# Down-projections of a hybrid decoder by seven block products for eight, with operands loaded stage by stage

## The chip, the cores and the metric

The kernel runs on one core of a Trainium2 chip. The metric is the time of one execution on the device in microseconds (us), the median over several runs; beside it one execution was profiled, and every row below is from that one.

Names of the engines: PE (TensorE) does matmuls, PEld is its weight load, DVE (VectorE) and ACT (ScalarE) do elementwise work, POOL is GpSimd, SP only issues DMAs here. The clock that PE was granted is given as a share of 2.4 GHz.

## The reference

A decoder trunk of two layers on one sequence of 1024 positions and 1024 channels, in float32. Layer 0 mixes tokens by two convolutional groups, layer 1 by stick-breaking attention with 16 heads. Each layer ends with a gated feed-forward block, which is what the change is about:

```python
D_FF = 2816                                   # 22 blocks of 128 channels
def conv_ffn(h, w_up, dw_w, dw_b, w_down):
    u = causal_dwconv(h @ w_up, dw_w, dw_b)   # width 3, along positions
    gate, val = jnp.split(u, 2, axis=-1)
    return (jax.nn.silu(gate) * val) @ w_down # (1024, 2816) @ (2816, 1024)

h = rmsnorm(x, ffn_norm_g[layer])
x = x + conv_ffn(h, ffn_w_up[layer], ffn_dw_w[layer], ffn_dw_b[layer], ffn_w_down[layer])
```

The last product is the down-projection. It runs once in each layer.

## The kernel before

**Precision.** PE multiplies in a reduced format, so each operand is split in a high and a low part: `split` (L421 to 429) casts on ACT (L426) and subtracts on DVE (L427). `mm3` (L439 to 444) then makes three matmuls of 512 columns, high x high, high x low, low x high, into one PSUM bank.

**Memory.** SBUF is managed as slots of 128 x 1024 floats (`Mem`): 16 low slots, which lie in the two buffers `hH` and `hL` and are free only while the normed input isn't needed, and 38 others; an allocation asks for one kind or the other. PSUM has eight banks of 512 columns: three double tiles (`bigs`) and two single ones (`sms`).

**Up.** `Up.block(f)`, for f from 0 to 21, computes gate and value of one block of 128 channels by seven block products for eight, adds the convolution, and multiplies (`post`, L387 to 408). The result, a tile of 128 channels x 1024 positions, is stored to DRAM (`hd[f]`, L406). So the transposed activations of the down-projection lie in DRAM, 22 tiles.

**Down.** `ffn` (L935 to 1004) cuts the 22 blocks in groups of 3, 5, 5, 5 and 4 (`GROUPS`). For each group it loads the activations of a block (L950) and its weight rows (L951), both 128 x 1024, and splits them. `back_tile` goes over the eight row tiles of 128 positions: for each it sums all blocks of the group into a double bank by 2 x 3 matmuls per block, and adds the sum to the residual tile `x[t]` with one DVE instruction of 1024 columns (L576). While one group is multiplied the next is loaded and split, one block per row tile. The last group goes through `back_all` (L579 to 607), which calls the next layer's `tail` after each row tile, or stores the output rows. The residual tiles come back from DRAM all at once, before the first group (L970).

**Order.** Outside the first stage and the attention the framework's scheduler orders each engine's instructions by the times that it estimates for them. Each engine, and SP's queue of DMAs, then runs strictly in that order: an instruction that waits holds up all behind it on its engine. A DMA on SP's queue waits for the slot that it writes to be free, so for the last reader of what was there.

## Time and profile before

| | us |
|---|---|
| median of 3 runs (lowest to highest) | 2390.34 (2389.73 to 2393.57) |
| profiled execution | 2388.36 |
| its span, first to last instruction | 2386.6 |
| PE busy | 2291.5, 11340 matmuls |
| DVE busy | 1612.6 |
| ACT busy | 1186.9 |
| POOL busy | 570.8 |

A row of the page's groups gives the line in the kernel, the engine, the operation, what it writes and reads, how often, the busy time in us, the mean of one in ns, and then the engine's idle time just before, with what ended it. A window gives for each engine the busy us in it. Matmuls overlap, so the busy time of one (some 390 ns) is longer than the distance from one to the next.

In time order: the convolutional mixer ends at about 380; Up of layer 0 lasts to about 780, its down-projection to about 1010; the attention follows, to about 1660; Up of layer 1 lasts to about 2120, its down-projection to the end. The passage from an Up to its down-projection is called the ramp below.

### The profile page before, as it was taken

How to read it: one execution, taken by the hardware profiler on the slowest of the kernel's cores; microseconds unless marked ns; L12 is line 12 of the kernel's file. 1: busy time of each engine (PE TensorE's matmuls, PEld its weight loads, DVE VectorE, ACT ScalarE, POOL GpSimd, SP SyncE). 2: the span in 40 equal slices, each digit the busy share in tenths (PEclk: the TensorE clock that was granted, in tenths of full speed). 3: DMA queues.
4: the chain of work that ended last, by engine and by line, in shares of the span. 5: the costliest groups of instructions: out<-in, count | busy, mean ns of one | idle time of the engine just before them, and what ended most of it. 6: DMA issues, size and time to landing. Idle time of an engine off the chain costs nothing.

```text
span 2386.6 us, 29571 instructions
## 1 busy us (share of the span) xinstructions
PE 2291.5 (96%) x11340; PEld 1958.7 (82%) x11340; DVE 1612.6 (68%) x1772; ACT 1186.9 (50%) x1882; POOL 570.8 (24%) x555
## 2 busy tenths in 40 slices
PE   8998998999999899999999999989899999999999
PEld 8886886888888788899899999878688888877887
DVE  6779458777766744246888888886867766766332
ACT  5442336565555421026677767764655555543110
POOL 2221113121111000025555555651311111200000
PEclk9999999999999999999999999999999999999999
DMA  5983044666665632211111110224466666646211
GB/s 170 190 177 92 27 137 106 171 148 141 166 159 146 220 129 93 61 54 27 36 27 36 36 36 10 86 83 146 106 150 150 155 150 154 145 149 250 71 36 71
DMA packets 225056, 268.43 MB, mean 112 GB/s; under 512 B 10013, under 2 KB 168209, under 8 KB 224913
## 3 DMA queue, kind: packets, MB, share of 16 engines
q1 hardware_dynamic: 194385, 201.61, 25.8%
q0 software_dynamic: 30528, 64.92, 16.1%
q8 instruction: 89, 1.46, 0.3%
q14 instruction: 54, 0.44, 0.1%
HBM read 158.07 MB, written 43.52 MB: 84 GB/s over the span
## 4 chain that ended last, share of the span: by engine, by line
PE 65%; DVE 15%; DMA 7%; ACT 5%; issue 5%; POOL 3%; DVEq 0%; SPq 0%; POOLq 0%; ACTq 0%
PE ps2b L442 7%; PE ps2b L444 7%; PE ps2b L443 7%; PE ps0b L442 6%; PE ps0b L444 6%; PE ps0b L443 6%; DMA t<-t 4%; PE ps0bb L443 3%; PE ps0bb L442 3%; PE ps0bb L444 3%; DVE t L1125 3%; DVE t L427 2%; PE ps1s L442 2%; PE ps1s L443 2%; PE ps1s L444 2%
## 5 line engine op out<-in xcount | busy, mean ns | idle before, releaser
L426 ACT CAST t<-t 128x1024 fp32r<-128x1024 f32 x242 | 249.2, 1048 | 329.8 <-DMA t<-t 76.0
L427 DVE TENSOR_TENSOR t<-t,t 128x1024 fp32r<-128x1024 f32 x238 | 300.5, 1276 | 96.0 <-ACT t L426 72.4
L201 POOL DMA_DIRECT2D t<-t x176 | 155.4, 965 | 679.0 <-DMA t<-in_ffn_w_up_dram 200.3
L617 DVE SCALAR_TENSOR_TENSOR t<-t,cst,t 128x1023 f32<-128x1023 f32 (+1 forms) x184 | 236.9, 1288 | 77.2 <-ACT t L615 71.3
L1125 DVE TENSOR_TENSOR_SCAN t<-t 128x127 f32<-128x127 f32 (+7 forms) x128 | 205.6, 1613 | 8.3 <-ACT t L1116 7.9
L442 PE MATMUL ps2b<-t,t 128*128 128x512 f32 x516 | 202.0, 392 | 6.7 <-ACT t L426 2.6
L443 PE MATMUL ps2b<-t,t 128*128 128x512 f32 x516 | 201.3, 390 | 0.5 <-DVE t L427 0.5
L444 PE MATMUL ps2b<-t,t 128*128 128x512 f32 x516 | 201.1, 390 | 0.0
L508 POOL TENSOR_TENSOR stat<-stat,mhalf 128x8 f32<-128x8 f32 (+1 forms) x65 | 80.7, 1242 | 399.5 <-DVE stat L507 399.4
L442 PE MATMUL ps1s<-wH,hH 128*128 128x384 f32 x448 | 165.3, 369 | 0.0
L444 PE MATMUL ps0b<-hH,t 128*128 128x512 f32 x396 | 154.9, 391 | 3.4 <-DVE t L427 3.4
L442 PE MATMUL ps0b<-hH,t 128*128 128x512 f32 x396 | 156.2, 395 | 1.4 <-ACT t L334 1.4
L443 PE MATMUL ps0b<-hL,t 128*128 128x512 f32 x396 | 155.1, 392 | 0.0
L444 PE MATMUL ps1s<-wH,hL 128*128 128x384 f32 x448 | 150.9, 337 | 0.0
L443 PE MATMUL ps1s<-wL,hH 128*128 128x384 f32 x448 | 150.5, 336 | 0.0
L1130 POOL TENSOR_TENSOR t<-t,t 128x639 f32<-128x639 f32 (+1 forms) x64 | 108.5, 1696 | 174.9 <-DVE t L1125 102.4
L442 PE MATMUL ps0b<-t,t 128*128 128x512 f32 x362 | 142.0, 392 | 3.5 <-DVE t L576 3.5
L443 PE MATMUL ps0b<-t,t 128*128 128x512 f32 x362 | 141.3, 390 | 0.0
L444 PE MATMUL ps0b<-t,t 128*128 128x512 f32 x362 | 141.2, 390 | 0.0
L615 ACT ACTIVATE t<-t,cst 128x1024 f32<-128x1024 f32 x88 | 109.3, 1242 | 43.4 <-DVE t L375 27.9
L1116 ACT ACTIVATE t<-ps1s 128x512 f32<-128x512 f32 (+1 forms) x192 | 95.5, 497 | 55.7 <-PE ps1s L1112 28.0
L442 PEld LDWEIGHTS ps2b<-t,t 128*128 128x128 f32 x516 | 96.8, 188 | 30.5 <-ACT t L426 3.4
(316 smaller groups left out, 5880.9 us busy)
## 6 DMA issues: line engine op xcount, KB each, us to landing
t<-in_ffn_w_up_dram SPq DMA_DIRECT2D x88, 512.0 KB
t<-t POOLq DMA_DIRECT2D x176, 256.0 KB, 4.0
hd<-t SPq DMA_DIRECT2D x44, 512.0 KB
t<-hd SPq DMA_DIRECT2D x44, 512.0 KB
t<-in_ffn_w_down_dram SPq DMA_DIRECT2D x44, 512.0 KB
xd<-t SPq DMA_DIRECT2D x24, 512.0 KB
t<-xd SPq DMA_DIRECT2D x24, 512.0 KB
wr<-in_attn_w_qkv_dram SPq DMA_DIRECT2D x24, 512.0 KB
```

The costliest lines, as they stand in the source:

```text
L201: nc.gpsimd.dma_start(out=out, in_=src, accum_op=ALU.add)
L426: nc.scalar.copy(out=r(m.ap(h)), in_=m.ap(src))
L427: (eng or nc.vector).tensor_tensor(out=r(m.ap(l)), in0=m.ap(src), in1=m.ap(h), op=ALU.subtract)
L442: mm(out=ps, lhsT=sH, rhs=mH, start=start, stop=False, skip_group_check=onto)
L443: mm(out=ps, lhsT=sH, rhs=mL, start=False, stop=False, skip_group_check=onto)
L444: mm(out=ps, lhsT=sL, rhs=mH, start=False, stop=stop, skip_group_check=onto)
L508: nc.gpsimd.tensor_tensor(out=ss, in0=ss, in1=self.mhalf[:, 0:count], op=ALU.pow)
L615: nc.scalar.activation(dst, src, AF.Identity, scale=wcols[2], bias=bias)
L617: nc.vector.scalar_tensor_tensor(out=dst[:, s:], in0=src[:, :S - s], scalar=wcols[2 - s], in1=dst[:, s:], op0=ALU.mult, op1=ALU.add)
L1116: nc.scalar.activation(K[:, c0:c1], ps, AF.Sigmoid, scale=-sc)
L1125: self.nc.vector.tensor_tensor_scan(out=rev, data0=rev, data1=rev, initial=1.0, op0=ALU.mult, op1=ALU.bypass)
L1130: self.nc.gpsimd.tensor_tensor(out=B[:, 0:n - 1], in0=B[:, 0:n - 1], in1=K[:, 1:n], op=ALU.mult)
```

## The change

The 22 channel blocks are taken as 11 pairs, positions and output columns in halves. A pair's contribution is then a product of 2 x 2 blocks, and is made by seven block products with sums of blocks as operands (Winograd's form of Strassen's method). All pairs sum into the same banks, so the combinations of the products are made once, over all pairs.

- **Activations.** `post` hands its tile to the new `store`. For an even block it stores the first half and keeps the tile; for the odd one it makes four half-size sums on DVE and stores three tiles. `hs[i]` holds seven half tiles for each pair, in the order in which they are used, 1.75 MB instead of 1 MB.
- **Weights.** The sums of weight blocks are made in the down-projection, on DVE, in one slot per pair that stays for three stages.
- **Stages.** `Down` walks 4 stages x 11 pairs, 44 steps. Stages 1 to 3 make two products a step (banks `a[t]` and `d[t]`, t from 0 to 3), stage 4 makes one. `a` keeps accumulating over all four stages; `d` starts anew in stages 1 and 3. After the last pair of stages 1, 2 and 3 the eight banks are added to halves of `x` (`add`), after stage 4 the four of `a`.
- **Flow.** `ahead` issues loads three steps ahead and preparations (sums, casts, splits) two steps ahead. The residual tiles are loaded one per step, in steps 4 to 11 of stage 1. Split operands lie in the low slots, four per step, in stages 1 to 3.
- **Tails.** Row tiles 0 to 3 are complete after stage 3, and their tails run in the first steps of stage 4; tiles 4 to 7 follow one by one at the end, for which the last six pairs are multiplied tile by tile. In layer 1 halves of rows are stored as they are complete.
- **Attention.** `qkv_piece` takes its first bank from the third double tile.

The core of the diff:

```diff
-GROUPS = [3, 5, 5, 5, 4]
...
-        nc.sync.dma_start(out=k.hd[f], in_=m.ap(v))
-        for s in (g, sg, v):
+        for s in (g, sg):
+            m.free(s)
+        self.store(f, v)
+    def store(self, f, v):
+        k, m, nc = self.k, self.k.m, self.k.nc
+        hs = k.hs[f // 2]
+        lo, hi = slice(0, 512), slice(512, 1024)
+        if f % 2 == 0:
+            nc.sync.dma_start(out=hs[:, 0:512], in_=m.ap(v)[:, lo])
+            self.even = v
+            return
+        q = [m.alloc() for _ in range(2)]
+        E, O, S12, S43 = [m.ap(s) for s in (self.even, v, *q)]
+        for out, x, y, op in ((S12[:, lo], E[:, hi], O[:, hi], ALU.add), (S12[:, hi], S12[:, lo], E[:, lo], ALU.subtract),
+                              (S43[:, lo], O[:, lo], S12[:, hi], ALU.subtract), (S43[:, hi], E[:, lo], E[:, hi], ALU.subtract)):
+            nc.vector.tensor_tensor(out=out, in0=x, in1=y, op=op)
+        for c, s in zip((512, 1536, 2560), (*q, v)):
+            nc.sync.dma_start(out=hs[:, c:c + 1024], in_=m.ap(s))
+        for s in (self.even, v, *q):
             m.free(s)
 
...
+class Down:
+    N = NF // 2
+    LOAD, PREP = 3, 2
+    OUTER = 5
...
+        self.steps = [(s, i) for s in range(4) for i in range(self.N)]
...
+        halves = [b[:, c:c + 512] for b in big for c in (0, 512)]
+        self.a, self.d = halves[0:4], halves[4:6] + sm
...
+    def load(self):
+        s, i = self.steps[self.nl]
+        self.nl += 1
+        k, m, sync = self.k, self.k.m, self.k.nc.sync
+        lo = slice(0, 512)
+        if s == 3 and i == 0 and self.l == 0:
+            m.held = set(range(NSLOT - NLAST, NSLOT))
+        n = 512 if s == 3 else 1024
+        a = m.alloc()
+        if s == 0:
+            self.w[i] = m.alloc(keep=True)
+        w = m.ap(self.w[i])
+        if s == 0:
+            sync.dma_start(out=w, in_=self.row0[i])
+        elif s == 1:
+            sync.dma_start(out=w[:, lo], in_=self.rows[i][3])
+        sync.dma_start(out=m.ap(a)[:, 0:n], in_=k.hs[i][:, s * 1024:s * 1024 + n])
+        b = None
+        if s == 2:
+            b = m.alloc()
+            sync.dma_start(out=w[:, lo], in_=self.rows[i][0])
+            sync.dma_start(out=m.ap(b)[:, lo], in_=self.rows[i][2])
+        self.raw[s, i] = a, b
+    def prep(self):
+        s, i = self.steps[self.np]
+        self.np += 1
+        k, m, nc = self.k, self.k.m, self.k.nc
+        lo, hi = slice(0, 512), slice(512, 1024)
+        a, b = self.raw.pop((s, i))
+        w = m.ap(self.w[i])
+        def sub(out, x, y):
+            nc.vector.tensor_tensor(out=out, in0=x, in1=y, op=ALU.subtract)
+        def split(src, ht):
+            h, l = m.alloc(ht), m.alloc(ht)
+            nc.scalar.copy(out=r(m.ap(h)), in_=src)
+            nc.vector.tensor_tensor(out=r(m.ap(l)), in0=src, in1=m.ap(h), op=ALU.subtract)
+            return h, l
+        def split_half(src):
+            s = m.alloc()
+            h, l = m.ap(s)[:, lo], m.ap(s)[:, hi]
+            nc.scalar.copy(out=r(h), in_=src)
+            nc.vector.tensor_tensor(out=r(l), in0=src, in1=h, op=ALU.subtract)
+            return s
+        if s == 3:
+            self.ops[s, i] = split_half(m.ap(a)[:, lo]), split_half(w[:, lo])
+            m.free(self.w.pop(i))
+        else:
+            x = split(m.ap(a), True)
+            if s == 0:
+                sub(w[:, hi], w[:, hi], w[:, lo])
+                y = split(w, True)
+            elif s == 1:
+                sub(w[:, hi], w[:, lo], w[:, hi])
+                y = split(w, True)
+            else:
+                B = m.ap(b)
+                sub(B[:, hi], w[:, hi], w[:, lo])
+                sub(w[:, lo], B[:, lo], w[:, hi])
+                y = split(B, True)
+                m.free(b)
+            self.ops[s, i] = (*x, *y)
+        m.free(a)
+    def products(self, s, i, t):
+        k, m = self.k, self.k.m
+        ops = [r(m.ap(o)) for o in self.ops[s, i]]
+        ts, lo, hi = slice(t * P, (t + 1) * P), slice(0, 512), slice(512, 1024)
+        first, last = i == 0, i == self.N - 1
+        if s == 3:
+            x, y = ops
+            k.mm3(self.a[t], x[:, ts], x[:, 512 + t * P:512 + (t + 1) * P], y[:, lo], y[:, hi], False, last, True)
+            return
+        xh, xl, yh, yl = ops
+        t2 = slice(512 + t * P, 512 + (t + 1) * P)
+        a, d = ((lo, hi), (hi, lo), (hi, lo))[s]
+        k.mm3(self.a[t], xh[:, ts], xl[:, ts], yh[:, a], yl[:, a], first and s == 0, last, s > 0)
+        k.mm3(self.d[t], xh[:, t2], xl[:, t2], yh[:, d], yl[:, d], first and s != 1, last, s == 1)
+    def add(self, t, c, ps):
+        x = self.k.m.ap(self.k.x[t])[:, c * 512:(c + 1) * 512]
+        self.k.nc.vector.tensor_tensor(out=x, in0=ps, in1=x, op=ALU.add)
...
+    def run(self):
+        k, m = self.k, self.k.m
+        k.x = [None] * NT
+        for n, (s, i) in enumerate(self.steps):
+            if s == 3 and i == self.OUTER:
+                break
+            self.ahead(n)
+            if s == 0 and i >= self.N - NT:
+                t = i - (self.N - NT)
+                k.x[t] = m.alloc(keep=True)
+                k.nc.sync.dma_start(out=m.ap(k.x[t]), in_=k.xd[t])
+            for t in range(4):
+                self.products(s, i, t)
+                if i == self.N - 1:
+                    to, c = ((0, 0), (0, 1), (4, 1))[s]
+                    self.add(t + to, c, self.a[t])
+                    to, c = ((4, 1), (0, 1), (0, 0))[s]
+                    self.add(t + to, c, self.d[t])
+            self.close(s, i)
+            if s == 2 and i == self.N - 1:
+                m.drop_ht()
+                if self.l:
+                    for t in range(4):
+                        self.tail(t + 4, slice(512, 1024))
+            if s == 3 and i < 4:
+                self.tail(i)
+        self.ahead(len(self.steps))
+        for t in range(4):
+            for i in range(self.OUTER, self.N):
+                self.products(3, i, t)
+            self.add(t + 4, 0, self.a[t])
+            if t == 3:
+                for i in range(self.OUTER, self.N):
+                    self.close(3, i)
+            if self.l == 0:
+                self.tail(t + 4)
+            else:
+                self.tail(t + 4, slice(0, 512))
...
+        down = Down(self, l, tail)
...
+                down.load()
...
+                down.load()
+                down.prep()
...
+        self.m.give_ht()
+        down.run()
...
-            self.qps = self.big()[:, 0:512] if p == 0 else self.qbs[t % len(self.qbs)]
+            self.qps = self.bigs[2][:, t % 2 * 512:(t % 2 + 1) * 512] if p == 0 else self.qbs[t % len(self.qbs)]
...
-            self.hd = [dp.tile([P, S], F32, name=f"hd{f}") for f in range(NF)]
+            self.hs = [dp.tile([P, 7 * 512], F32, name=f"hs{i}") for i in range(NF // 2)]
```

SP's queue of DMAs in the ramp of layer 0, before: `hd` and `xd` are the activations and residual tiles in DRAM, the number behind a name tells the tile (`hd_108` is block 0).

```order
L970 DMA t_5615<-xd_100 128x1024
L406 DMA hd_128<-t_5472 128x1024
L970 DMA t_5617<-xd_101 128x1024
L951 DMA t_5709<-in_ffn_w_down_dram 128x1024
L950 DMA t_5708<-hd_114 128x1024
L970 DMA t_5619<-xd_102 128x1024
L970 DMA t_5621<-xd_103 128x1024
L950 DMA t_5735<-hd_115 128x1024
L951 DMA t_5736<-in_ffn_w_down_dram 128x1024
L970 DMA t_5623<-xd_104 128x1024
L970 DMA t_5625<-xd_105 128x1024
L951 DMA t_5632<-in_ffn_w_down_dram 128x1024
```

The same place after: `hs_108` is pair 0, L475 loads activations, L472 the weights of stage 1, L474 a half row of weights for stage 2, L567 a residual tile.

```order
L475 DMA t_6130<-hs_113 128x1024
L474 DMA t_5543<-in_ffn_w_down_dram 128x512
L475 DMA t_5715<-hs_112 128x1024
L475 DMA t_6322<-hs_108 128x1024
L472 DMA t_5887<-in_ffn_w_down_dram 128x1024
L475 DMA t_5956<-hs_108 128x1024
L472 DMA t_5678<-in_ffn_w_down_dram 128x1024
L472 DMA t_5716<-in_ffn_w_down_dram 128x1024
L567 DMA t_5895<-xd_103 128x1024
L472 DMA t_5922<-in_ffn_w_down_dram 128x1024
L475 DMA t_6162<-hs_114 128x1024
L474 DMA t_5674<-in_ffn_w_down_dram 128x512
```

Before, residual tiles and the next blocks' operands alternate. After, among the loads of stage 1 stand those of later stages: `t_6130` and `t_6162` are activations of stage 2, `t_6322` of stage 3, and L474 writes a slot (`t_5543`, `t_5674`) that the stage 1 split of the same weights must have read.

DVE between two groups before: L576 adds a double bank to a row tile, L427 is the subtraction of a split.

```order
L427 TENSOR_TENSOR t_6358<-t_6287,t_6357 128x1024
L576 TENSOR_TENSOR t_5615<-ps0bb_559,t_5615 128x1024
L427 TENSOR_TENSOR t_6362<-t_6288,t_6361 128x1024
L576 TENSOR_TENSOR t_5617<-ps0b_71,t_5617 128x1024
L576 TENSOR_TENSOR t_5619<-ps0b_72,t_5619 128x1024
L576 TENSOR_TENSOR t_5621<-ps0bb_559,t_5621 128x1024
L576 TENSOR_TENSOR t_5623<-ps0b_71,t_5623 128x1024
L576 TENSOR_TENSOR t_5625<-ps0b_72,t_5625 128x1024
L576 TENSOR_TENSOR t_5627<-ps0bb_559,t_5627 128x1024
```

DVE at the end of stage 2 of layer 0 after: L551 adds one bank to half a row tile, L498 is the subtraction of a split, L493 a sum of weight blocks.

```order
L498 TENSOR_TENSOR hL<-t_6356,hL 128x1024
L498 TENSOR_TENSOR hL<-t_6358,hL 128x1024
L493 TENSOR_TENSOR t_6681<-t_5922 128x512
L493 TENSOR_TENSOR t_5922<-t_6681,t_5922 128x512
L551 TENSOR_TENSOR t_5790<-ps0b_71,t_5790 128x512
L498 TENSOR_TENSOR hL<-t_6391,hL 128x1024
L551 TENSOR_TENSOR t_5790<-ps0bb_548,t_5790 128x512
L498 TENSOR_TENSOR hL<-t_6393,hL 128x1024
L551 TENSOR_TENSOR t_5860<-ps0b_72,t_5860 128x512
L551 TENSOR_TENSOR t_5825<-ps0b_71,t_5825 128x512
L551 TENSOR_TENSOR t_5860<-ps0bs_549,t_5860 128x512
```

Eight adds of 512 columns stand where adds of 1024 columns were, in a place where all eight banks end together, with splits for stage 3 between them.

## Rows read from the trace of the kernel before

**Rows 1.** The page, part 1: busy us of each engine, share of the span, instructions.
```profile
PE 2291.5 (96%) x11340; PEld 1958.7 (82%) x11340; DVE 1612.6 (68%) x1772; ACT 1186.9 (50%) x1882; POOL 570.8 (24%) x555
```

**Rows 2.** Windows by stage; x counts the instructions that touch a window.
```profile
core 0: us, PE busy (x) PEld busy (x) DVE busy (x) ACT busy (x) POOL busy (x), PEclk, DMA share, GB/s
400.00:775.00 375.00, 374.72 (x1652) 309.23 (x1651) 265.53 (x256) 216.64 (x274) 66.44 (x76) 1.00 0.65 155
1740.00:2115.00 375.00, 373.64 (x1643) 307.60 (x1642) 265.05 (x256) 214.44 (x273) 66.24 (x76) 1.00 0.65 153
780.00:840.00 60.00, 53.37 (x229) 42.11 (x228) 47.43 (x42) 29.04 (x31) 0.00 (x0) 1.00 0.66 243
2115.00:2180.00 65.00, 59.59 (x256) 47.31 (x255) 50.86 (x46) 32.27 (x35) 0.00 (x0) 1.00 0.62 225
850.00:1000.00 150.00, 150.00 (x664) 124.20 (x663) 49.27 (x44) 19.99 (x24) 0.00 (x0) 1.00 0.17 59
2190.00:2370.00 180.00, 180.00 (x796) 149.08 (x795) 53.57 (x45) 18.23 (x18) 0.00 (x0) 1.00 0.14 51
```

**Rows 3.** Waits of TensorE in the two ramps: us in total, times, longest us.
```profile
PE ps0b L442 <- DVE t L576: 3.5, 3, 1.6
PE ps0bb L442 <- ACT t L426: 2.6, 2, 1.9
...
PE ps2b L442 <- ACT t L426: 2.6, 2, 1.9
PE ps2b L442 <- DVE t L576: 1.6, 2, 1.3
```

**Rows 4.** Groups by line: DVE and ACT in 780:840, then TensorE in 850:1000.
```profile
L427 DVE TENSOR_TENSOR t<-t,t 128x1024 fp32r<-128x1024 f32 x11 | 13.2, 1220 | 1.3 <-ACT t L426 1.3
L576 DVE TENSOR_TENSOR t<-ps0b,t 128x1024 f32<-128x1024 f32 x5 | 6.1, 1222 | 0.4 <-DMA t<-xd 0.4
L380 DVE TENSOR_TENSOR t<-t,t 128x512 f32<-128x512 f32 x1 | 0.7, 686 | 0.0
...
L426 ACT CAST t<-t 128x1024 fp32r<-128x1024 f32 x12 | 12.6, 1047 | 12.5 <-DMA t<-hd 4.3 <-DVE hH L427 3.2 <-DVE t L405 3.1
...
L442 PE MATMUL ps0b<-t,t 128*128 128x512 f32 x72 | 28.0, 389 | 0.0
```

**Rows 5.** Windows of 10 us, a DMA issue group of the page, a wait of SP.
```profile
770.00:780.00 10.00, 10.00 (x46) 8.28 (x45) 5.32 (x6) 3.94 (x4) 0.00 (x0) 1.00 0.07 27
790.00:800.00 10.00, 8.57 (x36) 6.79 (x37) 4.02 (x4) 1.44 (x2) 0.00 (x0) 1.00 0.32 110
810.00:820.00 10.00, 10.00 (x46) 8.28 (x45) 9.69 (x10) 6.75 (x7) 0.00 (x0) 1.00 0.99 386
2180.00:2190.00 10.00, 10.00 (x45) 8.27 (x45) 7.59 (x7) 3.66 (x4) 0.00 (x0) 1.00 1.02 410
...
t<-t POOLq DMA_DIRECT2D x176, 256.0 KB, 4.0
...
SPq L406 <- DVE t L405: 196.9, 41, 9.1
```

**Rows 6.** Timeline of the last row tile: start, length, engine, instruction.
```profile
2378.16 0.39 PE L444 MATMUL ps2b<-t,t 128*128 128x512 f32 x1
...
2378.58 0.69 DVE L602 TENSOR_TENSOR t<-ps2b,t 128x512 f32<-128x512 f32 x1 [1.49 <-PE ps2b L444]
2379.33 0.50 PE L442 MATMUL ps2b<-t,t 128*128 128x512 f32 x1 [0.78 <-DVE t L602]
```

**Rows 7.** The longest wait of TensorE in 375:405, and windows around it.
```profile
PE ps0bb L443 <- DVE t L427: 6.2, 1, 6.2
...
384.00:388.00 4.00, 0.49 (x1) 0.17 (x1) 4.00 (x3) 2.83 (x4) 4.00 (x2) 0.97 0.00 0
388.00:392.00 4.00, 1.33 (x3) 1.14 (x4) 4.00 (x3) 1.35 (x2) 1.53 (x1) 0.50 0.00 0
392.00:396.00 4.00, 4.00 (x14) 3.13 (x14) 3.82 (x5) 0.96 (x2) 0.00 (x0) 0.68 0.44 129
```

More of the change, by code (lines that the diff above doesn't have):

```diff
@@ L40 @@
 NLAST = 9
-GROUPS = [3, 5, 5, 5, 4]
-FILL = 2
 MOVED_TAPS = 10
@@ L414, in close, with __init__, ahead @@
                     self.k.m.free(s)
+class Down:
+    N = NF // 2
+    LOAD, PREP = 3, 2
+    OUTER = 5
+    def __init__(self, k, l, tail):
+        self.k, self.l, self.tail = k, l, tail
+        self.w, self.raw, self.ops = {}, {}, {}
+        self.steps = [(s, i) for s in range(4) for i in range(self.N)]
+        self.nl = self.np = 0
+        big, sm = k.bigs, k.sms
+        halves = [b[:, c:c + 512] for b in big for c in (0, 512)]
+        self.a, self.d = halves[0:4], halves[4:6] + sm
+        wd = k.a["ffn_w_down"][l]
+        self.rows = [[wd[f * P:(f + 1) * P, c:c + 512] for f in (2 * i, 2 * i + 1) for c in (0, 512)] for i in range(self.N)]
+        self.row0 = [wd[2 * i * P:(2 * i + 1) * P, :] for i in range(self.N)]
+    def load(self):
[60 more added lines that the diff above has]
+        m.free(a)
+    def ahead(self, n):
+        while self.nl < min(n + self.LOAD + 1, len(self.steps)):
+            self.load()
+        while self.np < min(n + self.PREP + 1, len(self.steps)):
+            self.prep()
+    def products(self, s, i, t):
[15 more added lines that the diff above has]
+        self.k.nc.vector.tensor_tensor(out=x, in0=ps, in1=x, op=ALU.add)
+    def close(self, s, i):
+        for o in self.ops.pop((s, i)):
+            self.k.m.free(o)
+    def run(self):
[36 more added lines that the diff above has]
+                self.tail(t + 4, slice(0, 512))
@@ L935, in ffn @@
     def ffn(self, l, tail):
-        m, nc = self.m, self.nc
         up = self.up
```

56 lines of the change are left out of this document (removed).

## The prediction

> **What bounds the kernel now.** I read the page's totals first, then windows by stage, then the waits of TensorE, then the durations. TensorE is busy for 96% of the span, and the next engine, DVE, for 68% [rows 1]. The windows show what that share is made of. Both Up stages run at 374.7 and 373.6 us busy of 375, and the inner parts of both down-projections at 150 of 150 and 180 of 180 us, with the granted clock at 1.00 [rows 2]. So in a down-projection every matmul taken away shortens the path, as long as nothing else becomes late. The exception is the passage from Up to down ("the ramp"): 53.4 of 60 us and 59.6 of 65 us are busy [rows 2]. TensorE loses 6.6 and 5.4 us there, in short waits, the longest of 1.9 us, for casts and for the adds that free PSUM [rows 3]. DVE is at 79% in those stretches and the DMA share at 0.66 and 0.62, against 0.17 and 0.14 later [rows 2]: that is the one place where other resources are nearly as full as TensorE.
>
> **The matmuls.** A down-projection is 22 channel blocks x 8 row tiles x 2 column halves x 3 = 1056 matmuls of 512 columns. The new one is 11 pairs x 4 tiles x 7 products x 3 = 924. So 132 go in each layer, 264 in all. In the steady stretch 796 start in 180 us, 0.2261 us each [rows 2]; the 389 ns of a single one [rows 4] overlap with their neighbours. 264 x 0.2261 = 59.7 us, all on the path: **-59.7**. Two blocks' products now go into one bank without further work, since a bank keeps accumulating from stage to stage.
>
> **DVE in steady state.** A split of a 128x1024 tile is a cast of 1.05 us on ACT and a subtraction of 1.22 us on DVE; a 128x512 tensor operation takes 0.69 us [rows 4]. A step of stage 1 or 2 needs two splits and one half-size subtraction: 2 x 1.22 + 0.69 = 3.1 us of DVE beside 24 matmuls = 5.4 us of TensorE. Stage 3 needs 3.8 of 5.4, stage 4 1.4 of 2.7. ACT needs 2.1 of 5.4. For a layer the splits, subtractions and 28 half-size adds sum to 145 us of DVE (before: 44 splits and 40 adds of 1.22 = 102.5) under 924 x 0.2261 = 209 us of TensorE. That is hidden, and costs nothing while DVE works ahead; preparation runs two steps ahead. Loads are 1.05 MB per 5.4 us step, 193 GB/s, where 386 and 410 GB/s were moved for 10 us at a time [rows 5]. Steady state: **0**.
>
> **The ramp.** Here the load queue matters. It is one in-order queue, and the new order puts far more into it before the first stage is fed: activations and half rows of stages 2 and 3 stand ahead of what the next steps of stage 1 need. From the weights of step 3 up to the activations of step 10 there are 40 transfers of 512 KB and 12 of 256 KB, 24.1 MB (layer 1: 23.3 MB). At 386 GB/s [rows 5] that is 62.5 us (60.4). In the order of TensorE 210 matmuls stand between the first products of these two steps, 47.5 us. So the queue is 15 us (13 us) longer than the work that it feeds. It may start earlier: the slot of the first of these transfers is freed 68 matmuls, 15.4 us, before step 3. If that lead is used in full, the ramp loses nothing, 12.0 us less than now. If none is used, both ramps wait 15 + 13 us, and the last load still has to land (4.0 us for a 256 KB transfer [rows 5], the nearest), be cast and subtracted (2.3 us): 40 us in all, 28 more than now. I take 13 us each, 26 - 12 = **+14**, nearer to the upper end, because the queue has waiting instructions in it: a half row may load only when the split of the same tile is done, and everything behind it waits. The same thing is visible before: the DMA share is 0.07 and 0.32 in 770 to 780 and 790 to 800, then 0.99 from 810 on [rows 5], so an early start was not used there; SP stood 197 us in all on stores that wait for DVE [rows 5]. Bounds -12 and +28.
>
> The rate of 386 GB/s comes from the 10 us window at 810, and the one at 2180 shows 410 [rows 5]. The Trainium skill's page "DMA: Bandwidth & Descriptors" (Specifications) gives a core about 358 GB/s as its share of HBM. By that figure 24.1 MB would take 67 us, 5 us more in each ramp, and the sum below would be 10 us later, an estimate from that page; the trace's windows exceed it, so I don't use it.
>
> **The ends of stages.** When stage 1, 2 or 3 ends, eight half-size adds take the sums out of the banks, 8 x 0.69 = 5.5 us, and TensorE may write a bank's neighbour half only when the add of the first half is done. In DVE's order splits of 1.22 us stand between these adds. What such a wait costs is visible in the last tile: the matmul starts at 2378.16, the add at 2378.58, the next matmul at 2379.33, 0.78 us late [rows 6]. TensorE has 5 to 13 other matmuls, 1.1 to 2.9 us, in between here, so I take 0.5 us for each of six ends, **+3**. Bounds 0 and 6 x 1.6 = 9.6, the longest wait for an add in a ramp [rows 3].
>
> **Up.** Eleven times per layer four half-size operations make the sums: 88 x 0.69 = 60.5 us more of DVE. DVE goes from 265.5 to about 292 of 375 us there (71% to 78%) [rows 2], below TensorE. Stores grow from 4 to 7 half tiles of 256 KB per pair, 0.79 MB in some 38 us, at a DMA share of 0.65 [rows 2]. TensorE now loses 0.3 and 1.4 us; I take **+2** for both, bounds 0 and +6 (four times today's loss). **The end:** the split add of the last tile goes (-0.8 [rows 6]), the last store stays 256 KB, and in layer 0 the weights of the attention load against a shorter last stage: **0**, bounds -1 and +3.
>
> **The sum.** -59.7 + 14 + 3 + 2 = -40.7 us. The profiled execution took 2388.4 us (span 2386.6); this gives 2347.7. The median of the runs is 2.0 us above the profiled one, so I forecast **2350 us**. With the bounds -12 and +28 for the ramp and the others within theirs, this case covers about 2338 to 2363.
>
> **Rivals.** (a) *The ramp is hidden.* The lead is used, the new adds fall beside other products, and only the matmuls show: 2390.3 - 59.7 = 2331, down to 2322 if the ramp's own 12 us go too, less what the adds cost; I take 2328 to 2338. For it: the loads stand three steps ahead. Against: today's ramp isn't hidden although its queue is half as long. (b) *The ramp is bound by the queue, and the clock falls.* At 384 to 392 a single wait of 6.2 us was followed by a granted clock of 0.50, the lower of the two levels (1.2 of 2.4 GHz), and four more us at 0.68 [rows 7]; some 3 us are lost with each. No lead used (+28), a fall in each ramp (+6) and +5 elsewhere: 2390.3 - 59.7 + 39 = 2370. Against: no wait in today's ramps is over 1.9 us and their clock is 1.00 [rows 2, 3]. (c) *Slower: a chain per step.* If a load could be issued only when the step before it gave up its slots, each step would last as long as the chain landing 4.0 + half-size subtraction 0.69 + cast 1.05 + subtraction 1.22 = 7.0 us instead of 5.4: 66 such steps x 1.5 = +101, so 2432. It is slower than now from 59.7 / 66 = 0.9 us per step. Against: the low-order slots hold four steps' operands, and the DMA share of 0.17 leaves room [rows 2]. (d) *Part of that chain,* 0.7 to 1 us a step, eats nearly the whole gain: about 2378 to 2395. That the change does not do what it says is excluded by the instruction order, which has 132 matmuls fewer per layer.
>
> **How the numbers follow.** Forecast (2338 to 2363) 0.62, (a) 0.15, (b) 2363 to 2378 0.14, (d) 0.05, (c) 0.04. From 2331 to 2373 leaves out (c), (d), about a third of (a) and of (b): some 2 in 10. Within 0.2%, 4.8 us (about what a measurement of this kernel can tell from no change), lies half of (d): 0.03. Slower: (c) and a little of (d), 0.04. Faster: 0.93.
>
> **What the profile after would show.** 11076 matmul records instead of 11340; TensorE idle for about 13 us in each ramp, released by casts and subtractions that wait for a DMA, with the DMA share at 0.9 or more; after that 100% busy up to the stage ends, with waits of about half a microsecond there. DVE should rise by about 60 us in Up and 85 us in the down-projections, to some 1758 us. Wrong would be: ramps that lose under 6 us (a), a clock under 1.00 in them (b), or waits in every step of stages 1 to 3 (c, d).

## The result and the profile after

The changed kernel takes **2359.0 us** (median of 4 runs, 2357.5 to 2361.8) against 2390.7 of the kernel before, a ratio of 0.9867 (95% interval 0.985 to 0.9884). It is faster, by 32 us where 40 were forecast; 9 us separate the time from the predicted 2350, and it lies inside both ranges (2331 to 2373, and 2338 to 2363 for the forecast alone). The profiled execution took 2357.5 us with a span of 2355.5, so the spans differ by 31.1 us.

The totals of the page after, part 1 and the count of transfers in part 2, stand against [rows 1]:

```profile
PE 2245.8 (95%) x11076; PEld 1917.0 (81%) x11076; DVE 1737.8 (74%) x2011; ACT 1256.4 (53%) x1970; POOL 573.4 (24%) x555
...
DMA packets 244499, 308.81 MB, mean 131 GB/s; under 512 B 12174, under 2 KB 170370, under 8 KB 244354
```

264 matmuls are gone, as they should be. PE is busy for only 45.7 us less, though, and its share of the span fell: some of the matmuls that are left became slower. DVE rose by 125 us, and 40 MB more were moved.

The windows answer [rows 2]: two of Up, two that cut the first ramp, one of layer 0's later stages, two of the second ramp and one of layer 1's later stages (columns as in [rows 2]: us, busy us by engine, granted clock, DMA share, GB/s).

```profile
400.00:775.00 375.00, 372.97 (x1636) 305.96 (x1635) 286.43 (x294) 214.15 (x270) 66.72 (x76) 1.00 0.68 169
1720.00:2095.00 375.00, 372.80 (x1638) 306.65 (x1637) 283.99 (x291) 213.39 (x270) 66.68 (x76) 1.00 0.68 167
780.00:830.00 50.00, 50.00 (x222) 41.39 (x221) 43.13 (x47) 24.84 (x29) 0.00 (x0) 1.00 0.92 350
830.00:860.00 30.00, 23.13 (x83) 18.08 (x82) 18.73 (x21) 9.68 (x10) 0.00 (x0) 0.83 0.90 345
870.00:925.00 55.00, 55.00 (x245) 45.53 (x244) 35.44 (x39) 20.62 (x21) 0.00 (x0) 1.00 0.38 120
2100.00:2136.00 36.00, 36.00 (x160) 29.83 (x159) 32.07 (x34) 18.66 (x22) 0.00 (x0) 1.00 0.88 326
2136.00:2156.00 20.00, 10.87 (x36) 8.40 (x36) 13.79 (x16) 7.24 (x7) 0.00 (x0) 0.74 1.03 412
2185.00:2250.00 65.00, 64.83 (x285) 53.32 (x284) 44.28 (x51) 22.41 (x23) 0.00 (x0) 1.00 0.37 116
```

The reader is to see three things. The stages themselves run at 55 of 55 and 64.8 of 65 us. The ramps begin well, 50 of 50 and 36 of 36 us, with the DMA share at 0.92 and 0.88; then they break off. And a busy PE isn't a fast one there: between 2136 and 2156 PE counts 10.87 us as busy for 36 matmuls, which take 8.2 us at 0.2267 each, because the granted clock is 0.74.

The waits of PE (line, tile, what was waited for: us in total, times, longest), first from 800 to 960, then from 2100 to 2290, answer [rows 3]. L497 is the cast of a split, L551 the half-size add.

```profile
PE ps0b L622 <- ACT hL L497: 4.1, 1, 4.1
PE ps0b L622 <- ACT hH L497: 2.8, 1, 2.8
PE ps0b L622 <- DVE t L551: 1.7, 2, 0.9
PE ps0bb L622 <- DVE t L551: 1.0, 2, 0.8
...
PE ps2b L622 <- ACT hL L497: 9.1, 1, 9.1
PE ps2b L622 <- DVE t L551: 3.1, 4, 1.5
PE ps2b L622 <- ACT hH L497: 2.8, 1, 2.8
```

Four waits for casts make 18.8 us, eight for adds 5.8. What stood before the longest is told by the chain of work that ended last, from 2120 to 2150 (start, us, what):

```profile
2136.75 10.15 DMA t<-in_ffn_w_down_dram
...
2146.92 0.70 DVE t L493
...
2147.65 1.05 ACT hL L497
```

A row of weights was issued at 2136.75 and took 10.15 us to land, among other transfers at a DMA share of 1.03 and 410 GB/s; then came the subtraction of the sum, the cast, and the matmul at 2148.74. This is the path of the forecast: the load queue, then a half-size subtraction and a cast. The row is the eighth of the eleven that stage 1 needs in this layer, and SP issued it as soon as PE gave its slot free (it waited 0.2 us for the matmul of 2136.51). So it wasn't issued late; it landed late. Ahead of it SP had issued 16 loads of activations where the seven steps before need 7, five half rows of weights for later stages, and six residual tiles, and the DMA share was 1.03 in the six us before.

**Where the 31 us are.** Matmuls of 512 columns start 0.2267 us apart when nothing is in the way (it is the distance of the records in a steady stretch; [rows 2] gave 0.2261 with its edges). So I add up, for each stretch, by how much the distance from one such matmul's start to the next exceeds that. Stretches are cut at the same matmuls in every kernel: the down-projection runs from its first product to the 1056th matmul (924th with the change) after it.

| lost by TensorE, us | Up 0 | Down 0 | Up 1 | Down 1 |
|---|---|---|---|---|
| before | 1.5 | 7.4 | 3.8 | 7.1 |
| after | 3.7 | 15.6 | 3.7 | 24.2 |

The two down-projections lose 39.8 us in place of 14.5, which is 25.3 more. Of the difference in span of -31.1, Down 0 has -20.7, Down 1 -12.9, Up 0 +2.5, Up 1 0.0, the pieces of work between the first down-projection and the attention +2.4, and the rest (the start, the attention, the end) -2.4.

The same sums at each place, after: the ramp of layer 0 7.1 + 4.4 = 11.5 us, that of layer 1 12.2 and some 4, so 27.5 to 28 in all, against 13.4 before (7.3 and 6.1; the last tile had the other 1.1). The ends of stages 1 and 2 lost 1.7 and 2.2 us in layer 0, some 1.2 and 6.5 in layer 1, those of stage 3 next to nothing: about 11.6 us.

**The clock.** Windows of 4 us around the longest wait and around the end of stage 2 in layer 1, which answer [rows 7]:

```profile
2144.00:2148.00 4.00, 0.00 (x0) 0.00 (x0) 2.78 (x3) 0.35 (x1) 0.00 (x0) 0.56 1.03 410
2148.00:2152.00 4.00, 3.25 (x8) 2.59 (x9) 1.92 (x2) 1.15 (x2) 0.00 (x0) 0.50 1.03 410
2152.00:2156.00 4.00, 4.00 (x14) 3.17 (x13) 1.23 (x1) 0.59 (x1) 0.00 (x0) 0.66 1.03 421
...
2254.00:2258.00 4.00, 2.02 (x6) 0.97 (x6) 4.00 (x6) 0.62 (x1) 0.00 (x0) 0.89 0.00 0
2258.00:2262.00 4.00, 3.84 (x9) 2.93 (x10) 4.00 (x7) 1.99 (x2) 0.00 (x0) 0.50 0.24 66
2262.00:2266.00 4.00, 4.00 (x14) 3.13 (x14) 2.69 (x4) 0.62 (x1) 0.00 (x0) 0.75 0.21 66
```

At the lower level (0.50, 1.2 of 2.4 GHz) 14 matmuls go into 4 us or fewer, where 18 go at 1.00. After the wait that ended at 2148.74 the slow matmuls cost 12.2 - 9.3 = 2.9 us, after that of 4.1 us in layer 0 7.1 - 4.2 = 2.9, after that of 2.8 us there 4.4 - 3.0 = 1.4, and at the stage end at 2255 6.5 less the three gaps of 1.6, 0.9 and 0.9, so 3.1 us.

**That stage end** in the timeline, DVE and PE (start, length, engine, instruction, in brackets the idle time and what ended it), which answers [rows 6]:

```profile
2253.96 0.68 DVE L551 TENSOR_TENSOR t<-ps2b,t 128x512 f32<-128x512 f32 x1
2254.56 1.21 DVE L498 TENSOR_TENSOR hL<-t,hL 128x1024 fp32r<-128x1024 f32 x1
2255.69 0.68 DVE L551 TENSOR_TENSOR t<-ps2b,t 128x512 f32<-128x512 f32 x1
2256.29 1.21 DVE L498 TENSOR_TENSOR hL<-t,hL 128x1024 fp32r<-128x1024 f32 x1
2257.42 0.68 DVE L551 TENSOR_TENSOR t<-ps2b,t 128x512 f32<-128x512 f32 x1
...
2254.69 0.50 PE L622 MATMUL ps2b<-hH 128*128 128x512 f32 x1 [1.47 <-DVE t L551]
2256.43 0.50 PE L622 MATMUL ps2b<-hH 128*128 128x512 f32 x1 [0.77 <-DVE t L551]
2258.16 0.80 PE L622 MATMUL ps2b<-hH 128*128 128x512 f32 x1 [0.67 <-DVE t L551]
```

Add, split, add, split, add: PE gets a bank every 1.73 us, and what it can do with one lasts 0.7 to 1 us. The third matmul already takes 0.80 us.

### The profile page after: what moved, and what is told of

It reads as the page before. It is cut to its first block, busy times and chain, and to the rows that moved or that the text cites. A ratio compares the mean times of both kernels' runs of the same rounds, so it can differ in the third digit from the quotient of the medians.

```text
span 2355.5 us, 29730 instructions
## 1 busy us (share of the span) xinstructions
PE 2245.8 (95%) x11076; PEld 1917.0 (81%) x11076; DVE 1737.8 (74%) x2011; ACT 1256.4 (53%) x1970; POOL 573.4 (24%) x555
## 5 line engine op out<-in xcount | busy, mean ns | idle before, releaser
L606 ACT CAST t<-t 128x1024 fp32r<-128x1024 f32 x186 | 192.5, 1048 | 235.0 <-DMA hs<-t 60.2
L607 DVE TENSOR_TENSOR t<-t,t 128x1024 fp32r<-128x1024 f32 x182 | 233.0, 1288 | 93.4 <-ACT t L606 42.7
L622 PE MATMUL ps2b<-t,t 128*128 128x512 f32 x342 | 133.8, 392 | 2.5 <-ACT t L371 1.9
L623 PE MATMUL ps2b<-t,t 128*128 128x512 f32 x342 | 133.4, 390 | 0.0
L624 PE MATMUL ps2b<-t,t 128*128 128x512 f32 x342 | 133.0, 390 | 0.0
L1274 ACT CAST t<-ps1s 128x512 fp32r<-128x512 f32 (+1 forms) x160 | 87.3, 545 | 61.9 <-PE ps1s L1270 54.1
L497 ACT CAST hH<-t 128x1024 fp32r<-128x1024 f32 x64 | 64.8, 1050 | 101.3 <-PE ps0b L623 24.5
L1275 DVE TENSOR_TENSOR t<-ps1s,t 128x512 fp32r<-128x512 f32 (+1 forms) x160 | 100.3, 628 | 21.1 <-ACT t L1274 18.6
L497 ACT CAST hL<-t 128x1024 fp32r<-128x1024 f32 x64 | 65.0, 1051 | 86.5 <-PE ps0bs L623 26.7
## 6 DMA issues: line engine op xcount, KB each, us to landing
t<-t POOLq DMA_DIRECT2D x176, 256.0 KB, 4.3
t<-in_ffn_w_down_dram SPq DMA_DIRECT2D x66, 256.0 KB
```

Of the source, the lines that this page charges most:

```text
L497: nc.scalar.copy(out=r(m.ap(h)), in_=src)
L606: nc.scalar.copy(out=r(m.ap(h)), in_=m.ap(src))
L607: (eng or nc.vector).tensor_tensor(out=r(m.ap(l)), in0=m.ap(src), in1=m.ap(h), op=ALU.subtract)
L622: mm(out=ps, lhsT=sH, rhs=mH, start=start, stop=False, skip_group_check=onto)
L623: mm(out=ps, lhsT=sH, rhs=mL, start=False, stop=False, skip_group_check=onto)
L624: mm(out=ps, lhsT=sL, rhs=mH, start=False, stop=stop, skip_group_check=onto)
```

## The experiments

Twelve kernels were run, each against the kernel before on the same chip. The two questions were what the ramps wait for, and what the other losses are. Losses are worked out as in the table above, from the profiled execution; in after, E3 and E6 to E9 this is the fastest of the kernel's four, in E1 the slowest. The kernel before took 2389.1 to 2391.3 us (medians) beside these runs.

| kernel | us, median | Up 0 | Down 0 | Up 1 | Down 1 |
|---|---|---|---|---|---|
| after | 2359.0 | 3.7 | 15.6 | 3.7 | 24.2 |
| E1 SP in program order | 2326.6 | 6.0 | 2.1 | 6.4 | 4.2 |
| E2 DVE in program order | 2362.7 | 5.8 | 18.4 | 5.0 | 19.5 |
| E3 both | 2329.7 | 5.3 | 1.3 | 3.3 | 4.0 |
| E4 as E1, no sums in Up | 2349.1 | 16.5 | 2.1 | 16.9 | 3.4 |
| E5 as E1, residual loaded twice | 2326.4 | 6.2 | 1.8 | 6.4 | 3.9 |
| E6 as E1, no adds at stage ends | 2320.6 | 4.6 | 0.2 | 4.5 | 0.1 |
| E7 as E1, other banks after Down 0 | 2325.0 | 3.8 | 2.1 | 3.8 | 5.1 |
| E8 as after, residual not loaded | 2343.3 | 4.0 | 2.7 | 3.8 | 15.3 |
| E9 as E1, PE in program order too | 2347.1 | 4.2 | 13.0 | 2.7 | 10.6 |
| E10 as E1, Up's stores by GpSimd | 2350.5 | 17.0 | 2.2 | 13.2 | 2.1 |
| E11 before, SP in program order | 2391.8 | 2.5 | 7.5 | 6.6 | 5.5 |
| E12 as E7, slots kept longer | 2423.0 | 61.4 | 2.0 | 50.3 | 3.8 |

How far can a loss be trusted? In Up of layer 0, to 770, all engines run the same instructions in the same order in after, E1 to E3 and E5 to E9, and the losses there go from 3.7 to 6.2 us. In Up of layer 1 after, E1 and E2 have one order, and lose 3.7, 6.4 and 5.0. So differences of up to 2.7 us in Up come and go where no edit has touched it.

**E1. The order of the load queue.** The framework can be told to keep one engine's instructions in the order of the program; here SP's, in the down-projection.

```diff
-        down.run()
+        with self.tc.manual_schedule(engines={mybir.EngineType.SP}):
+            down.run()
```

> Edit: SP issues the DMAs of the new down-projections in the order in which the program names them (step by step), not in the order of the scheduler. Theory Q (what stands ahead in the queue): the two ramps lose about 13 and 18 us because transfers for stages 2 and 3 stand ahead of those of stage 1 while the DMA share is 1.03. In program order the eight steps of the ramp need 8 x 1.05 MB of operands and 4.2 MB of residual tiles, 12.6 MB, 31 us at 410 GB/s beside 43 us of products, so the waits of 4.1, 2.8 and 9.1 us go, the clock stays at 1.00, both ramps together lose under 8 us and the time is 2335 to 2344. Rival C (a chain of slots: load, cast, subtraction, products, load): the order doesn't matter, ramps lose about the same, 2355 to 2363. Rival S (strict order stalls SP on slots that are not free yet, and stages 2 and 3 are fed late): waits in every step, 2365 to 2385.

2326.6 us (2323.1 to 2329.1), ratio to the kernel before 0.973 (0.9706 to 0.9755), so 32 us less than the changed kernel, more than the theory asked for. Windows of both ramps, which stand against those after:

```profile
786.00:820.00 34.00, 34.00 (x152) 28.16 (x151) 29.11 (x31) 14.63 (x18) 0.00 (x0) 1.00 0.54 184
820.00:880.00 60.00, 59.22 (x262) 48.74 (x261) 46.87 (x54) 25.67 (x26) 0.00 (x0) 1.00 1.03 394
2130.00:2200.00 70.00, 69.13 (x305) 56.88 (x304) 57.46 (x67) 30.71 (x31) 0.00 (x0) 1.00 0.99 385
```

The DMAs are as full as after, 1.03 of their time for 60 us, and PE runs through it at 59.2 of 60 us and a clock of 1.00. The 23.6 MB that move from 820 to 880 (394 GB/s x 60 us) are the amount of the forecast's queue; they only come in the order in which they are wanted. No wait for a cast is left in the down-projections; the waits that remain are for adds:

```profile
PE ps0bs L622 <- DVE t L551: 0.8, 1, 0.8
PE ps0b L622 <- DVE t L551: 0.6, 1, 0.6
...
PE ps2b L622 <- DVE t L551: 2.3, 3, 1.7
PE ps2s L622 <- DVE t L551: 0.9, 1, 0.9
```

Theory Q holds; the chain of slots (C) and the stall of a strict queue (S) fall. In layer 1 SP now issues 7 loads of activations, one residual tile and no half row of a later stage ahead of the eighth weight row of stage 1, and the DMA share in the ten us before is 0.52. All of the ramps' 28 us are gone; the stage ends lose some 6 us in place of 11.6, a gain that the theory had not counted.

One reservation: the edit names SP alone, but the framework then orders the other engines anew. Of 11076 matmuls 316 stand in another place than in the changed kernel, of 2011 DVE instructions 219 and of 1970 on ACT 71, in the down-projections and in the pieces of work behind the first. The ramps' part is tied to SP's queue by the waits, which were waits for landings; what the other orders gave, at the stage ends above all, isn't told apart.

**E5. More bytes, right order.**

```diff
                 k.nc.sync.dma_start(out=m.ap(k.x[t]), in_=k.xd[t])
+                extra = m.alloc()
+                k.nc.sync.dma_start(out=m.ap(extra), in_=k.xd[t])
+                m.free(extra)
```

> Base: SP in program order (2326.6 us). Edit: in steps 4 to 11 of stage 1 every residual tile is loaded a second time, into a slot that nothing reads: 4.2 MB more in each ramp, 10.5 us at 400 GB/s. Theory Q (the order in the queue decides, not the bytes): the extra bytes push back only loads of stage 2, which are three steps, 16 us, early; both ramps lose under 3 us more, 2326 to 2333. Rival M (the ramp is bound by bytes): 10 us more in each ramp, and perhaps the clock falls again, 2345 to 2356.

2326.4 us, the same as E1. In 820 to 880 PE is busy for all 60 us while the DMA share is 1.02:

```profile
820.00:880.00 60.00, 60.00 (x266) 49.67 (x266) 44.15 (x49) 26.25 (x26) 0.00 (x0) 1.00 1.02 392
2130.00:2200.00 70.00, 69.00 (x303) 56.30 (x302) 52.78 (x60) 30.16 (x30) 0.00 (x0) 1.00 1.02 396
```

Here a full queue costs nothing as long as what stands at its head is what is needed next.

**E8. Fewer bytes, the order of the scheduler.**

```diff
+        self.seen = set()
...
-                k.nc.sync.dma_start(out=m.ap(k.x[t]), in_=k.xd[t])
...
-        self.k.nc.vector.tensor_tensor(out=x, in0=ps, in1=x, op=ALU.add)
+        if (t, c) in self.seen:
+            self.k.nc.vector.tensor_tensor(out=x, in0=ps, in1=x, op=ALU.add)
+        else:
+            self.seen.add((t, c))
+            self.k.nc.vector.tensor_copy(out=x, in_=ps)
```

> Base: the changed kernel itself, SP in the scheduler's order (2359.0 us). Edit: the residual tiles are not loaded in the new down-projections (8 transfers of 512 KB fewer in each ramp); the first sum for each half row tile is copied instead of added, so the residual is missing from the result. Theory M' (in the scheduler's order the ramp is bound by bytes: DMA share 1.03 from 800 to 850): 4.2 MB fewer are 10.5 us per ramp, the waits of 4.1, 2.8 and 9.1 us and the slow clock after them shrink to under 3 us in all, 2336 to 2346. Rival O (the queue stands at loads whose slots are not free, whatever the bytes): the long waits stay, 2352 to 2360.

2343.3 us, but with a spread from 2336 to 2352 that is wider than that of any other kernel here. In the profiled execution, with 2336.3 us the fastest of the four, the first ramp loses nothing, and the second still has one long wait:

```profile
PE ps2b L626 <- ACT hL L498: 4.9, 1, 4.9
PE ps2b L627 <- DVE hL L499: 0.7, 1, 0.7
```

So with nearly the same order (24 of the 533 other DMAs of SP stand elsewhere) the bytes count: in this execution 4.2 MB fewer in a ramp remove 11.5 us in layer 0 and some 7 in layer 1. By the medians the edit gives 15.7 us, half of E1's 32, so in the other executions less is removed. Theory M' holds for layer 0 of the profiled execution; for layer 1 it is right in sign and too large. E1, E5 and E8 together say what the ramps wait for: a long queue and, in it, an order in which loads of later stages stand in front. To set the order right is enough; to take bytes away gives about half.

**E11. The order without the change.** In the kernel before, the residual tiles and the loads of the groups are put in program order in the same way (the block from L968 on is put into the `manual_schedule` of E1).

> Base: the kernel before (2390 us). Edit: SP issues the DMAs of the old down-projections in the order in which the program names them: the eight residual tiles first, then the operands of the groups one after another. Theory (the old ramps are short of nothing but some waits of 0.7 to 2 us for casts and adds): at most their 15 us are to be had, 2378 to 2390, so the order is worth little without the seven-for-eight products. Rival (the order is worth as much as in the changed kernel, 32 us): 2360.

2391.8 us, ratio 1.0004 (0.9995 to 1.0014): no change. Its ramps lose what they lost before. The 32 us of E1 belong to the queue that the change made.

**E2 and E3. DVE in program order,** in stages 1 to 3, alone and with SP.

```diff
+        order = ExitStack()
+        order.enter_context(k.tc.manual_schedule(engines={mybir.EngineType.DVE}))
         for n, (s, i) in enumerate(self.steps):
+            if s == 3 and i == 0:
+                order.close()
```

> Edit: in stages 1 to 3 DVE runs in the order in which the program names the instructions; SP's queue stays with the scheduler. Theory A (splits between the adds): the six stage ends lose about 11 us together, 6.5 of them at one end in layer 1, because splits of 1.2 us stand between the eight adds; in program order the adds stand together, the ends lose 3 to 5 us, the time is 2350 to 2354 and the ramps stay as they are. Rival B (the adds themselves, 8 x 0.69 us, are what TensorE waits for): no change, 2357 to 2361. Rival D (strict order holds splits back behind adds and so makes the next stage's operands late): 2362 to 2375.

> Edit: both of the above, SP and DVE in program order in the new down-projections (DVE in stages 1 to 3). If ramps and stage ends are separate losses, the gains of the two single edits add: 2328 to 2338 by theories Q and A. If the ramps' loss by DVE hides behind that by the DMAs, the sum is less than that of both: 2338 to 2350.

In E3, as in E9 below, SP too is in program order in stages 1 to 3 only; in E1 it is in all four. E2 takes 2362.7 us, E3 2329.7, neither better than its base. At the stage ends the theory is borne out: the ends of stages 2 and 3 lose 0.4 us each in E2 and E3, where the changed kernel lost 2.2 and 6.5 at the ends of stage 2. But E2's ramps and the end of stage 1 beside them lose more, 17.5 and 18.7 us in all, with single waits of 4.8, 4.5 and 10.8 us:

```profile
PE ps0b L627 <- ACT hH L498: 6.5, 2, 4.8
PE ps0b L627 <- DVE t L552: 4.6, 2, 4.5
...
PE ps2b L627 <- ACT hL L498: 10.8, 1, 10.8
PE ps2b L627 <- DVE t L552: 3.3, 2, 3.1
```

DVE waits there for late operands (3.2 and 1.1 us for casts just before the adds that PE waits 4.5 us for), and in a strict order the adds wait behind it. In E3 the operands come in time, and the down-projections lose 5.3 us in place of E1's 6.3; the time doesn't show it, since other stretches differ by as much. Whether the DVE order is worth that 1 us isn't settled.

**E6. Without the adds at the ends of stages.**

```diff
-                if i == self.N - 1:
+                if i == self.N - 1 and s > 3:
```

> Base: SP in program order (2326.6 us). Edit: the adds at the ends of stages 1, 2 and 3 are left out (48 adds of 512 columns), so the result is not the reference's; the banks are begun anew without waiting for DVE. Theory A (the adds are what the stage ends wait for): the five short waits of 0.8 to 1.9 us that stand there in the base go, 2320 to 2323. Rival (those waits come from operands of the next stage that are late): 2325 to 2328.

2320.6 us (2316.7 to 2323.0), 6 us under E1, as expected. The two down-projections lose 0.3 us in all: they run without a single gap. Their lengths are 205.9 and 218.8 us, where those before had 242.7 and 256.0 with 7.4 and 7.1 lost. So without the losses a down-projection is 29.6 and 30.2 us shorter, and all of the price of E1's stage ends is waiting for adds.

**E9. PE in program order,** to have the banks end one after another.

```diff
...
+        order.enter_context(k.tc.manual_schedule(engines={mybir.EngineType.SP, mybir.EngineType.PE}))
...
```

> Base: SP in program order (2326.6 us). Edit: TensorE too runs stages 1 to 3 in the order of the program: in the last step of a stage the six products of a row tile stand together, where the scheduler leaves the last product of all banks to the end, so that all eight adds come at once. Theory P: with banks that end one after another, 1.4 us apart for two adds of 0.69, the adds keep pace and the stage ends lose nothing: 2320 to 2323, as without the adds (2320.6). Rival (strict order makes TensorE wait for the low half of an operand that it could have left to later): waits in the ramps, 2328 to 2345.

2347.1 us, just above the rival's range, and not by its mechanism. There are new waits at the start of the ramps (losses of 3.2, 0.8 and 0.8 us in layer 0), but none is for the low half of an operand: PE waits there for ACT's copies out of PSUM (L381, L376 and L372, 3.0, 0.7 and 0.7 us), with which the last block of Up empties its banks. And the stage ends don't vanish: 5.1 us at the first, 2.2 at the second, with matmuls that wait 0.76 and 1.79 us for L552. Theory P falls. Why the stage ends stay, isn't shown; that two banks of one double tile count as one tile for waits is a possible reason, and it wasn't tried apart.

**E7. The banks of the pieces after Down 0.** The change gave the pieces of the attention's first weights the two halves of one double tile by turns.

```diff
-            self.qps = self.bigs[2][:, t % 2 * 512:(t % 2 + 1) * 512] if p == 0 else self.qbs[t % len(self.qbs)]
+            if p:
+                self.qps = self.qbs[t % len(self.qbs)]
+            elif t < 5:
+                self.qps = self.bigs[2][:, t % 2 * 512:(t % 2 + 1) * 512]
+            else:
+                self.qps = self.bigs[t - 5][:, 0:512]
```

> Base: SP in program order (2326.6 us). Edit: the last three of the eight pieces of the first attention weights take their banks from three different double tiles instead of the two halves of one. Theory: after the down-projection of layer 0 TensorE waits three times, 2.3 us in all, for the instruction that empties the other half of the same double tile, since a wait is per tile; with separate tiles these waits go, 2323 to 2325. Rival (the pieces wait for the normed rows anyway): no change, 2325 to 2328.

2325.0 us (2322.5 to 2328.4) against 2326.6, inside each other's spread, so the time alone doesn't settle it. The trace does: with the two halves PE waited for L1171 or L1172, which empties the other half, two times in the changed kernel (1.9 us) and three times in E1 (2.3 us); in E7 no such wait is left, and the stretch of 600 matmuls in which they stand takes 101.5 us in place of 104.4 (102.8 before, 105.2 after).

**E4, E10 and E12. Up.** These three looked for the 3 to 6 us that Up loses.

Each has E1's edit besides. E4, in `store`:

```diff
...
-            nc.vector.tensor_tensor(out=out, in0=x, in1=y, op=op)
-        for c, s in zip((512, 1536, 2560), (*q, v)):
+        for c, s in zip((512, 1536, 2560), (self.even, v, v)):
...
-        for s in (self.even, v, *q):
+        for s in (self.even, v):
```

E10, so for both stores:

```diff
-            nc.sync.dma_start(out=hs[:, c:c + 1024], in_=m.ap(s))
+            nc.gpsimd.dma_start(out=hs[:, c:c + 1024], in_=m.ap(s))
```

E12, where the four slots are freed at the next even block:

```diff
-        for s in (self.even, v, *q):
-            m.free(s)
+        self.stored = (self.even, v, *q)
...
```

> Base: SP in program order (2326.6 us). Edit: the four sums of activation halves that Up makes for each pair are left out, the stores keep their number and bytes but send the unsummed tiles, so the result is not the reference's. Up loses 6.5 and 6.4 us of TensorE time in the base, against 0.9 and 2.7 in the kernel before. Theory V (DVE's 60 us of sums delay the work that frees PSUM banks): Up falls back to about 1 and 3 us, the time to 2317 to 2321. Rival T (the stores, 7 half tiles for 4, hold up the loads on SP's queue): Up stays at about 6 us each, 2324 to 2329.

> Base: SP in program order in the down-projections (2326.6 us). Edit: the stores of Up's half tiles are issued by GpSimd, not by SP. Theory W (a store waits on SP's queue for DVE, 95 us in Up of layer 0, loads and later stores stand behind it, and casts wait for slots that are still to be stored): Up loses 1 to 3 us in place of 6.4, 2317 to 2322. Rival G (GpSimd's queue now stands on DVE and its own transfers for the operands come late): Up loses more, 2330 to 2345.

> Base: SP in program order and the three double tiles for the last pieces of the attention weights (2325.0 us). Edit: the four slots whose content Up stores for a pair go back to the list of free slots one block, some 17 us, later. Theory L (casts of Up wait for slots that are still being stored: ACT 65 us and DVE 42 us in 32 waits, against 25 us in the kernel before): those waits go, Up loses 1 to 3 us in place of about 5 in each layer, 2317 to 2322. Rival (those waits of ACT and DVE are covered, TensorE's waits in Up come from DVE's sums): no change, 2323 to 2328.

All three went the wrong way. (The table puts the loss of E1's Up at 6.0 and 6.4 us, that of the kernel before at 1.5 and 3.8, so E4's expectation started a little too far apart.) E4 has 88 DVE instructions fewer and loses 10 us more in each Up; nothing in the two theories explains that, and its order of instructions and use of slots differ from E1's in more than the sums. Its trace shows ACT's splits in Up of layer 0 (400 to 790) waiting 54.1 us for transfers of GpSimd, where E1 has 2.5. E10 loses 7 to 11 us more, by waits for ACT's copies out of PSUM, on an ACT whose splits waited 52 us for slots that were still being stored, where E1 has 32 (PE from 400 to 790, then ACT there):

```profile
PE ps0bb L622 <- ACT t L375: 8.5, 6, 2.4
...
ACT t L606 <- DMA hs<-t: 51.9, 7, 9.4
```

E12 answers more than it was asked. The waits for slots that are being stored are all gone (in E7: ACT 65.2 us, DVE 41.5 us at the splits), and yet Up is 58 and 47 us longer, with many short waits for casts and for copies out of PSUM (PE, 400 to 836):

```profile
PE ps0bs L629 <- ACT t L613: 11.1, 4, 4.3
PE ps0b L629 <- DVE t L374: 9.2, 2, 5.0
PE ps0b L629 <- ACT t L376: 5.1, 5, 1.2
```

The waits moved: ACT's splits wait 40.8 us for transfers of GpSimd from 400 to 790, as in E4. Four of 38 slots kept for one block more cost some 100 us, so Up has no slot to spare. What Up's 3 to 6 us come from is not settled, and up to 2.7 us of them, as said, vary from execution to execution.

## Why the prediction was nearly right

- **Matmuls, -59.7: right.** 264 went, and E6, in which nothing else is lost, gives 29.6 and 30.2 us per layer.
- **DVE in steady state, 0: right.** Between the ramps and the ends PE never waits. DVE rose by 125 us, not 145: consecutive instructions of 0.69 us start 0.60 us apart in the timeline, so counting by the length of one was too much (239 more instructions x 0.09 us are an estimated 21).
- **The ramps, +14: right in size, the mechanism right, its make-up not.** They lose some 14 us more than before. The cause is the one of the forecast, loads of later stages ahead in an in-order queue (what SP had issued ahead of the longest wait, E1, E5 and E8 bear it out); in the 60 us from 800 to 860 the DMAs moved 22.6 MB, where the forecast had 24.1 MB in 62.5 us. The figure of 358 GB/s that the Trainium skill's page "DMA: Bandwidth & Descriptors" (Specifications) gives is passed here too: 410 GB/s in the windows around the longest wait, 394 over 60 us in E1. But I had 13 us of waits in each ramp and a clock of 1.00. The waits are 6.9 and 11.9 us, and the clock fell to 0.50 after them, the part that I had given to rival (b) and had named as a sign that the forecast is wrong. The two errors cancelled, which is luck: 7 us too much of waits, and some 9 for the slow matmuls and restarts that I had left out, of which 1.4 stood in the ramps before (13.4 by this count, 12.0 by the waits). [rows 7] had shown the fall, and a forecast with waits of 13 us should have had it.
- **"Nearer to the upper end, because the queue has waiting instructions in it": half right.** E5 shows that the queue's length alone harms nothing. It is what stands at its head.
- **Stage ends, +3: this term was mis-sized; it is 11.6.** The eight banks end together, add and split alternate on DVE, so at the worst end, that of stage 2 in layer 1, a bank comes free every 1.73 us and not every 0.69, and the clock fell there too (6.5 us lost). With DVE in program order, so with no split between the adds, the ends of stages 2 and 3 lose 0.4 us each (E2, E3). The order of after had shown these splits between the adds; I priced one wait of 0.5 us from the last tile, where no split stands between. The bound of 9.6 was passed too.
- **Up, +2: not contradicted** (+2.5 and 0.0 in the length of the stretches), but one order of instructions varies by as much from execution to execution, and the reason isn't known.
- **The end, 0:** the last tile's 1.05 us of [rows 6] went, as said. **Missing from the sum** is the stretch between Down 0 and the attention, +2.4: the line on `qkv_piece` stood in the change and got no price. E7 shows its waits.

Together: the two down-projections gave 33.6 us where 42.7 were forecast, 9.1 less; the pieces took 2.4, and Up 0.5 more than the 2 that it was given; the rest of the program gave 2.4 back, and no run says why. So 40.7 became 31.1. The state that rival (a) describes exists: the ramps can be hidden, and E1 does it with the same bytes. Rivals (c) and (d) fall with the steady stages, which show no wait in each step.

The fastest kernel here is E7, 2325.0 us (ratio to the kernel before 0.9725, 0.9707 to 0.9744), faster than both the kernel before and the changed one. Its down-projections still lose 7 us, at the ends of stages.

## What to carry to other kernels

Where loads go through one in-order queue, ask not only how many bytes stand in it but in which order: loads for later, put ahead early, stood in the way of 28 us in the two stretches here where the DMAs were full, and keeping the program's order on that one queue was worth as much as the seven-for-eight itself. Keeping it on other engines was not. Price a hand-over of all banks at once with the instructions that stand between the adds, and give each wait that is longer than those of today the slow clock that came after such waits elsewhere in the trace, as a price that may or may not fall due.

## What the runs showed of the hardware

A transfer of 512 KB took 10.15 us to land while the DMAs were at 1.03 and 410 GB/s. The transfers overlapped: SP issued one about every 1.3 us meanwhile. E5 kept 392 GB/s for 60 us beside a PE without a gap. The rate of the two windows of 10 us in [rows 5] was sustained: 394 GB/s over 60 us in E1, 411 over 30 us after (12.33 MB from 2120 to 2150).

The length of a wait doesn't tell by itself whether the clock falls after it. Three waits in a row of 1.5, 0.8 and 0.7 us, at the end of stage 2 in layer 1, were followed by a granted clock of 0.50, and three of 1.3, 0.8 and 0.8 at the same place in E8 by 1.00. A single wait of 1.9 us in the ramps of [rows 3] was followed by 1.00, and so was one of 3.0 us in E9, but one of 1.7 us in E2 by 0.60. In E9 the end of stage 1 has the same two waits in both layers, 0.76 and 1.79 us, 4.1 us apart; the windows just after them (the first in layer 0, the second in layer 1) differ in the clock, the last value but two:

```profile
867.00:870.00 3.00, 3.00 (x9) 2.32 (x9) 3.00 (x6) 1.26 (x2) 0.00 (x0) 0.57 1.05 399
2182.00:2186.00 4.00, 3.65 (x16) 3.04 (x17) 4.00 (x7) 2.00 (x2) 0.00 (x0) 1.00 1.03 397
```

What makes the difference, no run here shows.
